# Convolution rows of all four channel blocks kept in float32 through attention, with most of their combinations made afterwards, and weight chains that begin three work units after their loads

## The chip, the cores and the metric

The program runs on one core of a Trainium2 chip. The metric is the device time of one execution in microseconds. The core has five engines with a queue each, and each works through its queue in the order in which the program was written: TensorE (PE in the profile, with its weight loads as PEld), VectorE (DVE), ScalarE (ACT), GpSimd (POOL) and SyncE (SP), which here only issues DMA transfers. An instruction that waits for another engine holds back everything behind it in its own queue.

## The reference

One layer of a hybrid encoder block on 1024 tokens of width 1024, in float32:

```
u = rms_norm(x, norm1_g)
q, k, v, cb, cc, ch, ga, gb = split(u @ w_in)        # 512 x 6, then 1024, 1024
y_a = neighbourhood_attention(norm(q), norm(k), v, rpb) @ w_attn_branch
y_b = (cb * conv3(cc * ch)) @ w_conv_branch          # 512 channels, width 3 along the tokens
x = x + (sigmoid(ga) * y_a + sigmoid(gb) * y_b) @ w_o
h = rms_norm(x, norm2_g) @ w_mlp_in
x = x + square(relu(h)) @ w_mlp_out
```

## The kernel before, in words

Every float32 operand of a large product is split into two half-precision parts, a high one and a low one, after a scaling by powers of two. A product takes three passes (high by high, high by low, low by high). For a weight this means a chain: load it, on ACT multiply by row gains and square it, sum the squares per partition on DVE, add the sums up over the partitions with a one-column matmul on PE (`all_sum`, L228 to L233), derive the scale on DVE with some small instructions (`pow2_half`), then write the high part on ACT and the low part on DVE. A chain is a generator, and each `yield` is a place where it may be set aside.

Several products save work by seven products in place of eight (`SEVEN`, `seven`). For these, the kernel forms seven sums and differences ("forms") of the four quarters of each operand, and each form is split into high and low.

The order of the instructions is written by the program itself, in stages:

- **Start (0 to about 155 us):** normalisation and the products V, Q and K.
- **Attention (to about 319 us):** 77 steps `k`. Between them PE works off the convolution products of four channel blocks, j = 0 to 3 (`conv_mms`, L1112), twelve of 128x512 each per gate and half. Each block's products are multiplied on DVE and ACT, three taps are summed (partly on POOL, L879 and L882), and the result is written to `CF` in float32 (`conv_post`). `CF` has two places, and the second half of the same tile `bT` (`STG`) holds split forms on the way to the DRAM buffer `bf`. After blocks 1 and 3, `conv_split` finds the scale of a pair and `conv_forms` makes the seven forms: the sums on POOL (L912, L928 to L937), the high parts on ACT, the low parts on POOL (L919), and transfers to `bf` (L922).
- **Gates and branches (from about 319 to 588 us):** `gate_units(n)` for eight gate blocks, `a_unit` for the attention branch, `ab(j)` for the seven products of the convolution branch, with its forms read back from `bf` into `bT` by `land` (L1441), four at a time.
- **w_o and the MLP (to the end).**

In the gate stage a **unit** (L238) writes a group of matmuls to PE's queue, mostly twelve of 512 columns, and then makes `steps` advances of the foreground generators (`fg`) and `ticks` advances of the background chains (`bg`). A tick advances the first chain of the list that doesn't answer that it waits; a chain can wait for a number of units after a mark (`apart`), so that its `all_sum` is written to PE's queue some units behind the instruction which makes its operand. `work` counts the columns of the matmuls written; 6144 of them are a unit of twelve matmuls. Where a chain isn't through when its weight is needed, `built` advances it with all these waits lifted.

The weights come through five buffers of 512 KB (`raw`), loaded in the order G0, A0, S1, B0, S2, A1, S3, B1, S4 and so on, where S is the weight of a gate block after the first, A and B those of the two branches. `load_upto` (L261) issues the next load when an earlier weight has been split. While `held` is one, a buffer is set aside for the first gate's products (`sgr`).

The chains by name: `largest` for A (a maximum, L364 to L374), `rows_scaled` (L1144), `squares` (L1153), `sum_of` (L1124 and L1125) and `scale_of` for S, `prep_b` (L1338) for B. `forms_sum` (L1270, POOL) and `parts` (L1288 high on ACT, L1284 low on DVE) make the split forms of a weight. `turn_s` (L1257) issues eight transposing transfers that the first gates need. `m_done` (L1387 to L1394) splits the merged product of a gate block.

Of the kernel before, what the change touches and what calls it, by code (L numbers as in the profile page):

```python
# [101 lines left out]
def encoder_block(ctx: ExitStack, tc: tile.TileContext, x, weights, cols, gqk, rel, masks, out):  # L102
# [160 lines left out]
    def load_upto(n):  # L263
        while loaded[0] < min(n - held[0], limit[0], len(loads)):
            ch, p = loads[loaded[0]]
            loaded[0] += 1
            t = rawp.tile([128, 1024], F32, name="raw")
            load_into(t[:, :ch.widths[p][0] * ch.widths[p][1]], ch, p)
            ch.raw.append(t)

    class Chunk:


        def __init__(self, kind, widths, tag, rows, half, more):
            self.kind, self.bank = kind, {"V": "o", "Q": "o", "K": "s", "C": "d"}.get(kind)
            self.tag, self.rows, self.widths, self.more = tag, rows, widths, more
            self.offs = []
            self.raw, self.ready, self.half, self.pool = [], more > 0, half, () if half is None else (1,)
            self.split = False
            self.fine, self.s = False, None  # L280
# [78 lines left out]
        def largest(self, rm, a, b):  # L359
            o = 0  # L360
            for p, (k, w) in enumerate(self.widths):
                while len(self.raw) <= p:
                    yield WAIT
                V.tensor_reduce(sc[:, at(rm, o, k)], self.raw[p][:, :k * w].rearrange("p (k w) -> p k w", k=k),  # L364
                                axis=AX, op=OP.max, apply_absolute_value=True)
                o += k
                yield
# [6 lines left out]
            V.tensor_copy(c, sc[:, a])  # L374
            if self.kind != "V":
                yield from apart(units[0], 3 if self.kind != "O" else 1 + (self is cO[1]))
# [471 lines left out]
    def conv_post(j, g, half, ps, d):  # L848
# [17 lines left out]
        while not d.get("taps"):  # L866
            yield
        o = CF[:, j % 2, 512 * half:512 * half + 512].rearrange("p (b r c) -> p b r c", b=4, r=16)
        V.tensor_tensor(o, p3, perm(d["cv"], half), op=OP.mult)
# [17 lines left out]
    BTF = BT.rearrange("p w j t -> p (w j t)")  # L887
    CF = BTF[:, :4096].bitcast(F32).rearrange("p (e t) -> p e t", e=2)
    STG = BTF[:, 4096:].rearrange("p (n w t) -> p n w t", n=4, w=2)
    SLOT = BTF.rearrange("p (n a w t) -> p n a w t", n=4, a=2, w=2)  # L890
    BF = dram.tile([128, 7, 2, 2, 512], F16, name="bf")
    cm, form_tail, formed = keep(2), [], [False] * 2

    def conv_split(j):
        a, e = j // 2, j % 2
        A.activation(STG[:, 3].rearrange("p w t -> p (w t)").bitcast(BF16), CF[:, e], AF.Square,
                     scale=sc[:, cConv[j].inv], accum_out=sc[:, at(cm, e)])
        yield
        if e == 0:
            return  # L900
        m, s, r = tmp(), tmp(), tmp(2)
        V.tensor_scalar(sc[:, m], sc[:, at(cm, 0)], sc[:, at(cm, 1)], 1e-36, op0=OP.add, op1=OP.max)
        yield
        yield from pow2_half(m, 14, s, at(rowsB, a))
        for i in range(2):
            mul(s, cConv[j - 1 + i].inv, at(r, i))
        form_tail.append(conv_forms(a, r))

    def conv_forms(a, r):

        for e in range(2):
            G.tensor_scalar(CF[:, e], CF[:, e], sc[:, at(r, e)], 1.0, op0=OP.mult, op1=OP.mult)  # L912
        (e0, e1), (o0, o1) = ([CF[:, e, 512 * h:512 * h + 512] for h in range(2)] for e in range(2))

        def hi(n, v):
            A.activation(STG[:, n, 0], v, AF.Copy)

        def lo(n, v):
            G.tensor_tensor(STG[:, n, 1], v, STG[:, n, 0], op=OP.subtract)  # L919

        def put(n, f):
            SP.dma_start(BF[:, f, a], STG[:, n])  # L922
        yield
        hi(0, o1), hi(1, e0), hi(2, o0)
        yield
        lo(0, o1), lo(1, e0), lo(2, o0)
        yield
        G.tensor_tensor(o1, e1, o1, op=OP.subtract)  # L928
        hi(3, o1)
        yield  # L930
        G.tensor_tensor(e1, e0, e1, op=OP.subtract)
        G.tensor_tensor(e0, o1, e0, op=OP.subtract)
        yield
        put(0, 3), put(1, 0), put(2, 1)
        lo(3, o1)
        yield
        G.tensor_tensor(o0, o0, e0, op=OP.add)  # L937
        yield
        hi(0, e1), hi(1, e0), hi(2, o0)
        put(3, 2)  # L940
        yield
        lo(0, e1), lo(1, e0)
        yield
        lo(2, o0)
        yield
        put(0, 5), put(1, 4)
        yield
        put(2, 6)
        formed[a] = True

# [177 lines left out]
    def scale_of(am, more, n=3):  # L1128
# [6 lines left out]
        return s, inv  # L1135

    def rows_scaled(ch, g):

        for i in range(2):
            while len(ch.raw) <= i:  # L1140
                yield WAIT
            for k in range(4):
                v = ch.raw[i].rearrange("p (n k c) -> p k n c", n=2, k=4)[:, k]
                A.activation(v, v, AF.Copy, scale=sc[:, at(g, 4 * i + k)])  # L1144
            yield
# [92 lines left out]
    V, A = nc.vector, nc.scalar  # L1238
    fg.extend(form_tail)
    solo[0] = False  # L1240
# [63 lines left out]
    def prep_s(n):  # L1304
# [6 lines left out]
        else:  # L1311
# [17 lines left out]
    def prep_b(j):  # L1329

        ch = cB[j]
        while not ch.raw or not formed[1]:
            yield WAIT
# [47 lines left out]
    def m_done(n):  # L1381

        m = sgr[0] if n == 0 else sgs[n][:, 0::2]
        hi, lo = (M[w][:, n].rearrange("p (h t) -> p h t", h=2) for w in range(2))
# [10 lines left out]
        merged.add(n)  # L1395
        if n == 0:
            held[0] = 0
            load_upto(done[0] + 5)

    def gate_units(n, tail=None):  # L1400
# [3 lines left out]
        if n == 0:  # L1404
            for half in (1, 0):
# [29 lines left out]

    ORDB = (1, 6, 2, 4, 5, 7, 3)

# [7 lines left out]
    def first_forms():  # L1445
        while not formed[1]:
            yield
        for g in range(4):
# [6 lines left out]
    def part(n, i):  # L1455

        return sgs[n][i] if n == 0 else sgs[n][:, i]

# [34 lines left out]
    def ab(j):  # L1493
# [3 lines left out]
        def post2():  # L1497
            V.tensor_tensor(z[0], ps[2], z[0], op=OP.add)
            times(n, 0)
# [12 lines left out]
        posts = {1: lambda: A.activation(z[0], ps[1], AF.Copy),  # L1512
                 6: lambda: V.tensor_tensor(z[1], ps[6], z[0], op=OP.add), 2: post2, 7: post7, 3: post3}

# [9 lines left out]
        if j == 0:  # L1524
            order = "bbb2bb3bb"
        o = 0
# [6 lines left out]
        pairs[0] = j + 1  # L1533

    fg.append(first_forms())
    bg.append(prep_s(1))
# [693 lines left out]
```

## Time and profile before

| | us |
|---|---|
| median of the timed runs | 1257.69 (1256.26 to 1257.75, 3 runs) |
| the profiled execution, its own time | 1257.09 |
| span from its first to its last instruction | 1255.3 |
| PE busy | 1198.5 (95%) |
| DVE busy | 956.7 (76%) |
| ACT busy | 777.6 (62%) |
| POOL busy | 504.0 (40%) |

Busy time counts an instruction's own duration. A row of the timeline gives the start, the time to the end of the merged instructions, the engine, the line, the operation, what it writes and reads, the number of instructions, and in brackets the idle time of the engine just before and what ended it. The granted clock is the share of full speed that TensorE was given. PE's durations overlap, since matmuls are pipelined: a group of twelve takes 2.75 us as a row and starts 2.59 us after the one before it.

### The profile page before, as it was taken

How to read it: one execution, taken by the hardware profiler on the slowest of the kernel's cores; microseconds unless marked ns; L12 is line 12 of the kernel's file. 1: busy time of each engine (PE TensorE's matmuls, PEld its weight loads, DVE VectorE, ACT ScalarE, POOL GpSimd, SP SyncE). 2: the span in 40 equal slices, each digit the busy share in tenths (PEclk: the TensorE clock that was granted, in tenths of full speed). 3: DMA queues.
4: the chain of work that ended last, by engine and by line, in shares of the span. 5: the costliest groups of instructions: out<-in, count | busy, mean ns of one | idle time of the engine just before them, and what ended most of it. 6: DMA issues, size and time to landing. Idle time of an engine off the chain costs nothing.

```text
span 1255.3 us, 17139 instructions
## 1 busy us (share of the span) xinstructions
PE 1198.5 (95%) x6248; PEld 577.1 (46%) x6248; DVE 956.7 (76%) x1775; ACT 777.6 (62%) x1241; POOL 504.0 (40%) x332
## 2 busy tenths in 40 slices
PE   8999999989767759999999999999999999999998
PEld 7444444445333324444447644444444444444444
DVE  7987788888455687687778765545637989999998
ACT  7774677777545753444677877778765673545430
POOL 5510022431723224030102475565557654464472
PEclk9999999999978879999999999999999999999999
DMA  7755546777544241523349455435565643526212
GB/s 259 207 148 107 116 105 129 157 172 133 128 160 156 67 156 63 168 101 126 144 78 175 159 202 185 145 133 185 180 234 216 244 183 137 199 101 251 72 63 102
DMA packets 168373, 189.62 MB, mean 151 GB/s; under 512 B 123616, under 2 KB 124128, under 8 KB 164192
## 3 DMA queue, kind: packets, MB, share of 16 engines
q1 hardware_dynamic: 168288, 188.52, 50.2%
q8 instruction: 49, 0.80, 0.3%
q14 instruction: 36, 0.29, 0.1%
HBM read 117.19 MB, written 41.42 MB: 126 GB/s over the span
## 4 chain that ended last, share of the span: by engine, by line
PE 81%; DVE 7%; ACT 5%; POOL 3%; issue 2%; DMA 1%; SPq 1%; POOLq 0%; DVEq 0%; ACTq 0%
PE ps_d L238 25%; PE ps_s L238 22%; PE ps_o L238 18%; PE ps_d L1112 6%; PE ps_d L671 2%; PE ps_d L720 2%; PE ps_s L720 2%; PE ps_s L671 1%; DVE w_s L1284 1%; PE ps_o L1093 1%; SPq L1257 1%; ACT w_s L1288 1%; PE ps_s L1017 1%; ACT raw L1144 1%; POOL raw L1356 1%
## 5 line engine op out<-in xcount | busy, mean ns | idle before, releaser
L238 PEld LDWEIGHTS <-ops 128*128 128x128 f16 x1356 | 132.5, 98 | 157.3
L238 PEld LDWEIGHTS <-w 128*128 128x128 f16 x1368 | 132.9, 98 | 139.4
L1112 PE MATMUL ps_d<-uT,w_ws 128*128 128x512 f16 x576 | 128.6, 381 | 0.0
L238 PE MATMUL ps_s<-ops 128*128 128x512 f16 (+1 forms) x528 | 119.7, 377 | 0.0
L238 PE MATMUL ps_d<-ops 128*128 128x512 f16 x480 | 110.1, 379 | 0.0
L2051 ACT ACTIVATE ops<-hf,sc 128x2048 f16<-128x2048 f32 x26 | 52.0, 1998 | 84.8 <-PE ps_s L238 37.7
L1270 POOL TENSOR_TENSOR tsum<-raw 128x512 f32<-128x512 f32 x28 | 48.2, 1739 | 139.1 <-PE ps_s L238 73.9
L238 PEld LDWEIGHTS <-w_s 128*128 128x128 f16 x588 | 57.8, 99 | 96.4 <-ACT mL L1338 18.1
L1629 POOL TENSOR_TENSOR as<-as 128x512 f32<-128x512 f32 x60 | 82.9, 1382 | 41.6 <-ACT as L1911 38.0
L1112 PEld LDWEIGHTS <-w_ws 128*128 128x128 f16 x576 | 54.7, 98 | 65.6 <-issue 1.9
L238 PE MATMUL ps_d<-u2T,w 128*128 128x512 f16 (+1 forms) x360 | 78.8, 368 | 0.0
L238 PE MATMUL ps_o<-ops 128*128 128x512 f16 (+1 forms) x348 | 78.6, 375 | 0.0
L1144 ACT ACTIVATE raw<-raw,sc 128x256 f32<-128x256 f32 x164 | 67.8, 493 | 16.4 <-DMA raw<-in_weights 14.7
L2053 DVE SCALAR_TENSOR_TENSOR ops<-hf,sc,ops 128x2048 f16<-128x2048 f32 x26 | 74.4, 2860 | 3.2 <-ACT ops L2051 2.2
L238 PE MATMUL ps_o<-u2T,w 128*128 128x512 f16 (+1 forms) x348 | 76.0, 368 | 0.0
L238 PE MATMUL ps_s<-u2x,w 128*128 128x512 f16 (+1 forms) x336 | 74.5, 371 | 0.0
L1288 ACT ACTIVATE w<-raw,sc 128x512 f16<-128x512 f32 (+1 forms) x28 | 24.6, 927 | 50.9 <-DVE sc L477 50.9
L1944 DVE TENSOR_TENSOR as<-ps_s,as 128x512 f32<-128x512 f32 x13 | 9.0, 691 | 57.9 <-ACT as L1963 57.9
L1489 POOL TENSOR_TENSOR sg<-sg 128x512 f32<-128x512 f32 x12 | 16.4, 1378 | 83.1 <-DVE sg L1479 60.5
L2067 POOL TENSOR_TENSOR raw<-raw 128x1024 f32<-128x1024 f32 x8 | 30.8, 3876 | 36.7 <-DVE ops L2061 36.7
L2025 POOL TENSOR_TENSOR t<-raw,w2x 128x1024 f32<-128x1024 f32 x6 | 18.8, 3138 | 61.8 <-DMA w2x<-in_weights 61.8
L238 PEld LDWEIGHTS <-mH 128*128 128x128 f16 x304 | 29.6, 98 | 30.4
(427 smaller groups left out, 2775.5 us busy)
## 6 DMA issues: line engine op xcount, KB each, us to landing
raw<-in_weights SPq DMA_DIRECT2D x89, 512.0 KB, 5.3
hs<-as SPq DMA_DIRECT2D x16, 1792.0 KB, 8.0
hf<-hs SPq DMA_DIRECT2D x26, 1024.0 KB, 6.4
bT<-bf SPq DMA_DIRECT2D x28, 512.0 KB, 4.6
w2x<-in_weights SPq DMA_DIRECT2D x16, 512.0 KB, 7.6
raw<-in_weights SPq DMA_DIRECT2D x16, 384.0 KB, 3.7
xt<-in_x SPq DMA_DIRECT2D x8, 512.0 KB, 11.0
gs<-s SPq DMA_DIRECT2D x4, 1024.0 KB, 4.5
```

The lines of the kernel that those rows point to most:

```text
L238: T.matmul(ps, l, r, start=a, stop=b)
L671: T.matmul(ps, UT[:, sa, k, b * 128:(b + 1) * 128], w, start=(kind, k) == ("hh", 0), stop=(kind, k) == ("hl", 7))
L720: T.matmul(vbank["q", b], UT[:, sa, k, b * 128:(b + 1) * 128], cQ.parts[:, sw, 512 * k:512 * k + 512], start=(k, n) == (0, 0), stop=(k, n) ...
L1112: T.matmul(ps, l, r, start=a, stop=b)
L1144: A.activation(v, v, AF.Copy, scale=sc[:, at(g, 4 * i + k)])
L1270: G.tensor_tensor(t[:, o], a, b, op=OP.add)
L1288: A.activation(o(0), w, AF.Copy, scale=sc[:, scale(n)])
L1629: sub.tensor_tensor(z[o], z[a], z[b], op=op)
L2025: G.tensor_tensor(T2[:, i], w12[i], w22[i], op=OP.add)
L2051: A.activation(P[:, 1, 0], hf, AF.Copy, scale=sc[:, Rs])
L2053: V.scalar_tensor_tensor(P[:, 1, 1], hf, sc[:, Rs], P[:, 1, 0], op0=OP.mult, op1=OP.subtract)
L2067: G.tensor_tensor(w11[i2], w11[i2], w12[i2], op=OP.add)
```

## The change

- `CF` takes the whole of `bT`: four float32 places, one for each block, that stay until attention is over. The scale rows of both pairs are kept (`crow`).
- Of the first pair's seven forms, three are made and stored during attention (`conv_early`), one high or low part at a time, in the space of the first K heads (`KS`). Two more sums are begun there.
- The other four forms of the first pair and all seven of the second are made after attention, in `conv_late`, as the first foreground generator of the gate stage: eleven high parts on ACT, fifteen tensor-by-tensor instructions on DVE (nine low parts, six sums), two low parts and two scalings on POOL, eleven transfers to `bf`. Their staging space is `zb` and a part of `M[1]`, and three of the four places of `zb` are used a second time.
- The chains of A, S and B begin only when three units of work have been written since their load was (`aged`); the wait between the sum and its `all_sum` grows from two units to three for S and from one to two for B, and for A it counts work in place of units.
- Eight ticks are made ahead of the gate stage (`tick(8)`).
- The first gate's products go to `sg`, and the set-aside raw buffer is given back at the end of `gate_units(0)` in place of the end of `m_done(0)`.
- The order of the convolution branch's products is 1 2 4 6 5 7 3 in place of 1 6 2 4 5 7 3, and in the first `ab` the two attention units come at places 3 and 5.

```diff
@@ load_upto @@
+            ch.when.append(work[0])
@@ Chunk.largest @@
-                while len(self.raw) <= p:
+                while len(self.raw) <= p or self.kind == "A" and not aged(self, p):
+            if self.kind == "A":
+                yield from apart(work[0], 3 * 6144, work)
@@ module level @@
-    CF = BTF[:, :4096].bitcast(F32).rearrange("p (e t) -> p e t", e=2)
+    CF = BTF.bitcast(F32).rearrange("p (e t) -> p e t", e=4)
+    KS = KD[:, 0:2].rearrange("p a w t -> p (a w t)").rearrange("p (n w t) -> p n w t", n=4, w=2)
@@ conv_early @@
+    def conv_early():
+        (e0, e1), (o0, o1) = quarters(0)
+        conv_scaled(0)
+        yield
+        yield
+        for i, v in enumerate((o1, e0, o0)):
+            hi(KS[:, i], v)
+            yield
+            lo(KS[:, i], v, G)
+            yield
+        G.tensor_tensor(o1, e1, o1, op=OP.subtract)
+        yield
+        G.tensor_tensor(e1, e0, e1, op=OP.subtract)
+        for i, f in enumerate((3, 0, 1)):
+            put(KS[:, i], f, 0)
+            yield
@@ conv_late @@
+    def conv_late():
+        zs = zb.rearrange("p n t -> p (n t)").bitcast(F16).rearrange("p (n w t) -> p n w t", n=4, w=2)
+        ms = M[1][:, 2:6].rearrange("p n (w t) -> p n w t", w=2)
+        (e0, e1), (o0, o1) = quarters(0)
+        V.tensor_tensor(e0, o1, e0, op=OP.subtract)
+        V.tensor_tensor(o0, o0, e0, op=OP.add)
+        conv_scaled(1)
+        hi(zs[:, 0], o1), hi(zs[:, 1], e1)
+        yield
+        (p0, p1), (q0, q1) = quarters(1)
+        V.tensor_tensor(zs[:, 0, 1], o1, zs[:, 0, 0], op=OP.subtract)
+        V.tensor_tensor(zs[:, 1, 1], e1, zs[:, 1, 0], op=OP.subtract)
+        hi(zs[:, 2], e0), hi(zs[:, 3], o0)
+        yield
+        lo(zs[:, 2], e0, V), lo(zs[:, 3], o0, V)
+        yield
+        put(zs[:, 0], 2, 0), put(zs[:, 1], 5, 0)
+        hi(ms[:, 0], q1), hi(ms[:, 1], p0), hi(ms[:, 2], q0)
+        yield
+        put(zs[:, 2], 4, 0), put(zs[:, 3], 6, 0)
+        formed[0] = True
+        lo(ms[:, 0], q1, V), lo(ms[:, 1], p0, G), lo(ms[:, 2], q0, G)
+        V.tensor_tensor(q1, p1, q1, op=OP.subtract)
+        yield
+        yield
+        V.tensor_tensor(p1, p0, p1, op=OP.subtract)
+        V.tensor_tensor(p0, q1, p0, op=OP.subtract)
+        hi(ms[:, 3], q1)
+        yield
+        put(ms[:, 0], 3, 1), put(ms[:, 1], 0, 1), put(ms[:, 2], 1, 1)
+        V.tensor_tensor(q0, q0, p0, op=OP.add)
+        hi(zs[:, 0], p1), hi(zs[:, 1], p0)
+        yield
+        lo(ms[:, 3], q1, V), lo(zs[:, 0], p1, V)
+        hi(zs[:, 2], q0)
+        yield
+        lo(zs[:, 1], p0, V), lo(zs[:, 2], q0, V)
+        yield
+        put(ms[:, 3], 2, 1), put(zs[:, 0], 5, 1)
+        yield
+        put(zs[:, 1], 4, 1), put(zs[:, 2], 6, 1)
+        formed[1] = True
@@ aged @@
+    def aged(ch, i):
+        return forced[0] or i >= len(ch.when) or work[0] >= ch.when[i] + 3 * 6144
@@ rows_scaled @@
-            while len(ch.raw) <= i:
+            while len(ch.raw) <= i or ch.kind == "S" and not aged(ch, i):
@@ prep_s @@
-            s, ch.inv = yield from scale_of(am, 9, 2)
+            s, ch.inv = yield from scale_of(am, 9, 3)
@@ prep_b @@
-        while not ch.raw or not formed[1]:
+        while not ch.raw or not rowed[0] or not aged(ch, 0):
-        s, ch.inv = yield from scale_of(am, 0, 1)
+        s, ch.inv = yield from scale_of(am, 0, 2)
@@ m_done @@
-        if n == 0:
-            held[0] = 0
-            load_upto(done[0] + 5)
@@ gate_units @@
-                A.activation(sgr[0][:, half], sgr[0][:, half], AF.Sigmoid)
-            return [sgr[0][:, 0], z[1], sgr[0][:, 1], z[3]]
+                A.activation(z[2 * half], sgr[0][:, half], AF.Sigmoid)
+            held[0] = 0
+            load_upto(done[0] + 5)
+            return sg
@@ ORDB @@
-    ORDB = (1, 6, 2, 4, 5, 7, 3)
+    ORDB = (1, 2, 4, 6, 5, 7, 3)
@@ first_forms @@
-        while not formed[1]:
-            yield
+        yield from conv_late()
@@ ab @@
-            order = "bbb2bb3bb"
+            order = "bb2b3bbbb"
@@ before the first gate @@
+    tick(8)
     fg.append(first_forms())
```

More of the change, by code (lines that the diff above doesn't have):

```diff
@@ L277, in __init__ @@
             self.offs = []
+            self.when = []
             self.raw, self.ready, self.half, self.pool = [], more > 0, half, () if half is None else (1,)
@@ L374, in largest @@
             V.tensor_copy(c, sc[:, a])
-            if self.kind != "V":
+            if self.kind == "A":
+                yield from apart(work[0], 3 * 6144, work)
+            elif self.kind != "V":
                 yield from apart(units[0], 3 if self.kind != "O" else 1 + (self is cO[1]))
@@ L867, in conv_post @@
             yield
-        o = CF[:, j % 2, 512 * half:512 * half + 512].rearrange("p (b r c) -> p b r c", b=4, r=16)
+        o = CF[:, j, 512 * half:512 * half + 512].rearrange("p (b r c) -> p b r c", b=4, r=16)
         V.tensor_tensor(o, p3, perm(d["cv"], half), op=OP.mult)
@@ L905, in conv_split @@
         for i in range(2):
-            mul(s, cConv[j - 1 + i].inv, at(r, i))
-        form_tail.append(conv_forms(a, r))
-    def conv_forms(a, r):
-        for e in range(2):
[L912 to L922, printed above, removed]
+            mul(s, cConv[j - 1 + i].inv, at(crow, i))
@@ new lines, in conv_split, with conv_scaled, hi, lo @@
+        if a == 0:
+            form_tail.append(conv_early())
+        else:
+            rowed[0] = True
+    def conv_scaled(a):
+        for e in range(2):
+            t = CF[:, 2 * a + e]
+            G.tensor_scalar(t, t, sc[:, at(crow, e)], 1.0, op0=OP.mult, op1=OP.mult)
+    def hi(t, v):
+        A.activation(t[:, 0], v, AF.Copy)
+    def lo(t, v, e):
+        e.tensor_tensor(t[:, 1], v, t[:, 0], op=OP.subtract)
+    def put(t, f, a):
+        SP.dma_start(BF[:, f, a], t)
+    def conv_early():
+        (e0, e1), (o0, o1) = quarters(0)
+        conv_scaled(0)
@@ L1238, in encoder_block @@
     V, A = nc.vector, nc.scalar
-    fg.extend(form_tail)
+    assert not form_tail and rowed[0]
     solo[0] = False
@@ L1455, in part @@
     def part(n, i):
-        return sgs[n][i] if n == 0 else sgs[n][:, i]
+        return sgs[n][:, i]
     def a_unit(n, half):
```

34 lines of the change are left out of this document (10 added, 24 removed).

## The prediction

> **What bounds the kernel now.** First the page's span, then the busy time by stages (columns: window, length, busy time of PE, PEld, DVE, ACT and POOL with counts, granted clock, DMA share, GB/s).
>
> ```profile
> span 1255.3 us, 17139 instructions
> ```
>
> ```profile
> 319.00:396.00 77.00, 52.55 (x230) 22.84 (x229) 40.28 (x78) 40.87 (x76) 30.97 (x25) 0.84 0.53 158
> 396.00:476.00 80.00, 60.62 (x266) 26.34 (x264) 58.40 (x126) 44.75 (x77) 27.00 (x21) 0.87 0.37 116
> 476.00:588.00 112.00, 111.88 (x520) 50.57 (x519) 83.09 (x161) 47.56 (x76) 29.21 (x24) 1.00 0.28 89
> ```
>
> PE is the bound, and from 476 to 588 it is full. From 319 to 476, in the stage that the change edits, it isn't: 113 of 157 us, at a granted clock of 0.84 and 0.87. So I read PE's timeline there next:
>
> ```profile
> 334.52 2.75 PE L238 MATMUL ps_d<-uT,w_s 128*128 128x512 f16 x12
> 355.07 0.16 PE L229 MATMUL ps_s<-ones 128*128 128x1 bf16 x1 [17.80 <-DVE ones L1125]
> 355.10 4.39 PE L238 MATMUL ps_d<-qD,w_s 128*128 128x512 f16 x12
> ...
> 381.88 1.47 PE L238 MATMUL ps_o<-bT,w_wb 128*128 128x512 f16 x6 [1.62 <-DMA bT<-bf]
> 388.37 0.16 PE L229 MATMUL ps_d<-ones 128*128 128x1 bf16 x1 [5.03 <-DVE ones L1125]
> 388.40 4.80 PE L238 MATMUL ps_s<-qD,w_wa 128*128 128x512 f16 x12
> ...
> 425.86 0.16 PE L229 MATMUL ps_s<-ones 128*128 128x1 bf16 x1 [6.61 <-DVE ones L374]
> 425.89 4.83 PE L238 MATMUL ps_o<-uT,w_s 128*128 128x512 f16 x12
> ...
> 440.96 1.46 PE L238 MATMUL ps_s<-bT,w_wb 128*128 128x512 f16 x6
> ...
> 459.08 0.16 PE L229 MATMUL ps_s<-ones 128*128 128x1 bf16 x1 [12.78 <-DVE ones L1125]
> 459.10 2.72 PE L238 MATMUL ps_d<-bT,w_wb 128*128 128x512 f16 x6
> 461.62 4.06 PE L238 MATMUL ps_s<-qD,w_wa 128*128 128x512 f16 x12
> ```
>
> Four of the five waits stand at a one-column `all_sum` (L229): it was written to PE's queue before DVE had made its operand, and ready products stand behind it. After each of these four, a group of twelve takes 4.06 to 4.83 us in place of 2.75, and one of six 2.72 in place of 1.46. Until 396 that makes 17.80 + 1.62 + 5.03 = 24.4 of waiting and 1.6 + 2.1 = 3.7 of slow groups, 28 together; after 396, 6.61 + 12.78 = 19.4 and 2.1 + 1.3 + 1.3 = 4.7, 24 together. Dense, the two stages would last 77 − 28 = 49 and 80 − 24 = 56 us. So **52 us** is all that can be had here. What was late in the wait of 17.80 is seen on ACT and in SP's queue:
>
> ```profile
> 349.17 1.70 ACT L1144 ACTIVATE raw<-raw,sc 128x256 f32<-128x256 f32 x4 [6.84 <-DMA raw<-in_weights]
> ...
> 353.00 0.71 ACT L1338 ACTIVATE mL<-raw,sc 128x512 bf16<-128x512 f32 x1
> ```
>
> ```profile
> 332.60 11.22 SPq L1257 DMA_TRANSPOSE uT<-gs  x8
> 343.91 0.52 SPq L922 DMA_DIRECT2D bf<-bT  x1
> 344.55 0.87 SPq L261 DMA_DIRECT2D raw<-in_weights  x2
> ```
>
> B0's squares (L1338) sat on ACT behind the row scaling of S2, which waited for a load that SP issued at 344.55, behind eight transposes. The wait of 12.78 is of another kind. There DVE was at work:
>
> ```profile
> 456.13 2.64 DVE L1284 SCALAR_TENSOR_TENSOR w_s<-gsum,sc,w_s 128x1024 f16<-128x1024 f32 x2
> 458.69 0.15 DVE L1124 TENSOR_REDUCE sc<-sc 128x1 f32<-128x2 f32 x1
> 458.87 0.16 DVE L1125 CAST ones<-sc 128x1 bf16<-128x1 f32 x1
> ```
>
> B2's sum lay behind the low parts of an S weight that isn't used before 476: a backlog, not a transfer.
>
> **The change, part by part.**
>
> *Ages and longer waits.* With `aged`, S2's scaling is written three units after its load, so B0's squares pass it; the `all_sum` of B and of S is written a unit later. A unit is 2.6 us, so DVE may now be 5.2 (B) or 7.8 us (S) behind PE. No instruction is added. Behind 476 I take them at nothing: PE's 111.88 of 112 covers DVE's 83.09. Without this cover they cost a forced chain, priced under D.
>
> *`tick(8)` and the raw buffer.* A0's split (326.00 in a row below) moves ahead of the gates, some 7 us sooner, and its successor's load with it; the fifth buffer is free at the end of the first gate, not after `m_done(0)`. But S1's two buffers are still read by POOL's four sums behind two scalings (1.2 us each, by the `bT` row below) and by a low part, so the next two loads stand on SP until some 9 us after the gates' start, ahead of the transposes.
>
> *The late forms.* Rows: the first gate stage for instructions on `bT` alone (busy PE, DVE, ACT, POOL), the stores' time to landing, and three of DVE:
>
> ```profile
> 319.00:396.00 77.00, 9.73 (x42) 0.00 (x0) 4.19 (x7) 14.65 (x12) 0.84 0.53 158
> ```
>
> ```profile
> bf<-bT SPq DMA_DIRECT2D x7, 256.0 KB, 4.7
> ```
>
> ```profile
> 326.00 4.66 DVE L332 SCALAR_TENSOR_TENSOR w_wa<-raw,sc,w_wa 128x256 f16<-128x256 f32 x4 [8.70 <-ACT w_wa L345]
> ...
> 383.79 0.69 DVE L1513 TENSOR_TENSOR zb<-ps_s,zb 128x512 f32<-128x512 f32 x1 [4.81 <-ACT zb L1512]
> 384.40 1.66 DVE L332 SCALAR_TENSOR_TENSOR w_wa<-raw,sc,w_wa 128x256 f16<-128x256 f32 x4
> ```
>
> POOL does twelve instructions of forms there now, 14.65 us; afterwards four, about 5. ACT does four high parts more, 4.19 / 7 = 0.6 each: 2.4. DVE gets fifteen, at 0.69 each 10.4 us. With both inputs in SBUF they have no clean row: below, 0.69; above, beside POOL, 0.69 + (4.66 − 1.66) / 4 = 1.44. I take 0.69, since POOL's own load falls by 10. So DVE has 40.28 + 10.4 = 50.7 us of work in a stage which dense would last 49: **DVE becomes the bound of the first stage**.
>
> Nor will it run through. The stores of `conv_late`'s fourth advance follow the transposes on SP, 9 + 2 (two loads) + 11.22 = 22 us after the gates' start, and land 4.7 later, at 27. ACT overwrites the same places of `zb` in the eighth advance, which it reaches at about 16 by its own work. It stands for eleven us, and DVE, which needs those high parts next, for some 7. Behind it on ACT are S2's scaling and squares and one more high part (6 us), on DVE the last low parts and then A1's column, ready at about 34. PE comes to A1's `all_sum` after eleven units, at 28.5. So **what is late next is A1's sum**, 5.5 us and a slow group of 1.6. The last forms are stored from 34, landed at 39 and read back, at the same 4.7, at 44; the first product that needs them stands after thirteen units, at 34 dense and at 41 behind this wait. It was at 53:
>
> ```profile
> 372.32 1.46 PE L238 MATMUL ps_d<-bT,w_wb 128*128 128x512 f16 x6
> ```
>
> I take 64 us for the first stage: 50.7 of DVE, 7 of its standing and 6 for its shorter waits on ACT and POOL. Bounds: 49 (dense) and 77 (nothing won).
>
> In the second stage DVE's 58.40 are above the dense 56. But five S weights were split between 319 and 476:
>
> ```profile
> L1284 DVE SCALAR_TENSOR_TENSOR w_s<-gsum,sc,w_s 128x1024 f16<-128x1024 f32 x10 | 13.7, 1389 | 4.2 <-ACT w_s L1288 4.2
> ...
> L1284 DVE SCALAR_TENSOR_TENSOR w_s<-raw,sc,w_s 128x1024 f16<-128x1024 f32 x5 | 7.4, 1482 | 0.9 <-ACT w_s L1288 0.9
> ```
>
> S5's is due only after gate 4, which begins at 476. With ages and longer waits its (13.7 + 7.4) / 5 = 4.2 us and what goes with it leave the stage: some 53 for 56, in bursts. I take 66 (bounds 56 and 80).
>
> The 4.66 speaks against the change: four low parts, each held up beside POOL. The Trainium skill (SBUF — State Buffer, Who interferes with whom) says why: a DVE instruction with two SBUF inputs and a GpSimd instruction that reads SBUF shut each other out for a whole instruction, whichever starts first. The row agrees with it. By that rule each of the fifteen can wait out one POOL instruction, but only eight run near them (two scalings, four sums of S1, two low parts), which keeps the loss below 8 × 1.2 = 10 us, where rival C has 11.
>
> *Attention.* There POOL makes thirteen instructions of the first pair's forms, and afterwards seven. PE's waits there on DVE's `sc`, from 232 to 319:
>
> ```profile
> PE ps_s L1017 <- DVE sc L97: 4.8, 3, 1.8
> ```
>
> At most 4.8 us go, and at least none, since the seven left still meet the taps and biases on POOL. I take 3. The `sg` tile and the order of the products cost nothing: the same instructions, under PE.
>
> **Sum.** 77 − 64 = 13, 80 − 66 = 14, attention 3: 30 us. The profiled execution took 1257.09 (its span and 1.8 around it), 0.6 below the median, so **1227 us**.
>
> **The rivals.**
>
> *B, all the waits go.* For it: all but one have one form, and 476 to 588 has none of it. DVE's 50.7 then set the first stage: 26 + 24 + 5 = 55 less, 1202. Against: the reuse of `zb`.
>
> *C, DVE is shut out.* The fifteen go at 1.44: 11 us more, the first stage lasts 75; half of that backlog goes over, the second lasts 72. With 2 from attention 12 less, 1245. For it: the 4.66. Against: eight POOL instructions fewer.
>
> *D, slower: chains run into force.* The place is `built(cS[2])` ahead of gate 2. Counted in units from the gates' start, with the ticks that each gives, S2's sum is written at 10, its `all_sum` at 13, its last low part by 16.5; gate 2 begins at 18.5. If B0's chain or a load not yet aged holds it for over two units, the waits are lifted and PE stands for the rest: scaling 2 × 1.70, squares 4 × 0.71, POOL's sums 4 × 1.2, high parts 7 × 0.6, slow group 2.1, 17 us in all. S2 and S3 both forced cost 34, more than the 30 won: 1261. For it: each of these chains grows by three or four units, with five buffers to feed them. Against: the count.
>
> *E, no effect.* Other sums of the same backlog stall PE as long: 1257.
>
> **How the numbers follow.** Forecast (1216 to 1238) 0.42, B 0.18, C 0.22, E 0.06, D 0.12. Faster by over 0.2% (2.5 us, what a measurement can tell from no change) is forecast, B and C, 0.82; same 0.06; slower 0.12. The range leaves out D, the far side of E and the end of B: 1204 to 1252.
>
> **What would show it.** Right: no wait near 17 us in the first gates, but one near 5 at A1's `all_sum` (operand of L374), with ACT idle on `bf` before it; DVE above 75% of the first stage; the first convolution product 41 to 45 us after the first gate's start, now 53; PE's waits on DVE in attention below 2. Wrong: DVE's form instructions stretched to 1.4 (C); an `all_sum` wait of over 10 just ahead of gate 2 or 3 (D); ACT not idle on `bf` at all (B).

## The result, and the profile after

The changed kernel takes 1241.36 us (median of 4 runs, 1240.20 to 1244.53), the kernel before, timed beside it, 1257.12: a ratio of 0.988, with an interval of 0.986 to 0.990. The forecast was 1227, its range 1204 to 1252. The sign was right; of the 30 us foreseen 16 came.

First the span of the changed kernel, then its busy time in the three stages (columns as in the prediction's table by stages; the stages begin 4, 11 and 22 us sooner than before).

```profile
span 1239.4 us, 17137 instructions
```

```profile
314.60:384.00 69.40, 54.07 (x226) 22.97 (x225) 51.51 (x89) 44.55 (x84) 20.68 (x17) 0.88 0.66 199
384.00:454.00 70.00, 58.54 (x267) 25.78 (x265) 49.64 (x110) 40.92 (x67) 25.73 (x20) 0.94 0.33 109
454.00:566.00 112.00, 108.96 (x494) 48.58 (x494) 82.91 (x172) 45.78 (x73) 30.85 (x25) 0.98 0.27 91
```

The stages are bounded by four rows of PE's timeline: the first product of the gates, of gate 2, of gate 4 and of w_o. In the kernel before they are

```profile
318.98 3.19 PE L238 MATMUL ps_o<-uT,w_ws 128*128 128x512 f16 x14
...
395.65 1.67 PE L238 MATMUL ps_d<-uT,w_s 128*128 128x512 f16 x7
...
475.95 2.32 PE L238 MATMUL ps_d<-uT,w_s 128*128 128x512 f16 x10
...
587.82 0.59 PE L238 MATMUL ps_s<-w_ws,mH 128*128 128x512 f16 x2
```

and in the changed kernel, with PE's longer waits between them:

```profile
314.65 5.34 PE L238 MATMUL ps_o<-uT,w_ws 128*128 128x512 f16 x24
...
333.56 0.16 PE L229 MATMUL ps_d<-ones 128*128 128x1 bf16 x1 [3.21 <-DVE ones L1169]
...
346.97 0.18 PE L229 MATMUL ps_d<-ones 128*128 128x1 bf16 x1 [1.35 <-DMA bf<-mL]
...
358.24 0.19 PE L229 MATMUL ps_s<-ones 128*128 128x1 bf16 x1 [3.24 <-DVE sc L232]
358.29 2.72 PE L238 MATMUL ps_d<-bT,w_wb 128*128 128x512 f16 x6
...
381.72 2.74 PE L238 MATMUL ps_d<-bT,w_wb 128*128 128x512 f16 x6 [7.53 <-DMA bT<-bf]
...
384.33 1.94 PE L238 MATMUL ps_o<-uT,w_s 128*128 128x512 f16 x8
...
425.09 0.16 PE L229 MATMUL ps_s<-ones 128*128 128x1 bf16 x1 [6.83 <-DVE ones L376]
...
453.97 5.28 PE L238 MATMUL ps_d<-uT,w_s 128*128 128x512 f16 x12 [4.12 <-DVE zb L1549]
...
477.96 2.75 PE L238 MATMUL ps_o<-uT,w_s 128*128 128x512 f16 x12 [2.27 <-DVE sg L1478]
...
571.89 0.59 PE L238 MATMUL ps_s<-w_ws,mH 128*128 128x512 f16 x2
```

| part | before, us | after, us | gain | foreseen gain |
|---|---|---|---|---|
| up to the gates | 318.98 | 314.65 | 4.3 | 3 |
| first stage | 76.7 | 69.7 | 7.0 | 13 |
| second stage | 80.3 | 69.6 | 10.7 | 14 |
| gate 4 to w_o | 111.9 | 117.9 | −6.1 | 0 |

The sum is 15.9, and the two profiled executions differ by 1257.09 − 1241.13 = 16.0. The waits of 17.80 and 12.78 us are gone, and smaller ones stand at other places. Two of those are at no sum at all: 7.53 us for a read-back of the convolution's forms (`bT`), and 4.12 us for DVE's reading of a PSUM bank at the start of gate 4.

How the 7.53 us come about is told by the chain that ended last, over this stretch (start, us, what; the longer pieces between the two ends):

```profile
354.18 3.75 DVE w_wb L1331 x3
...
357.99 3.56 DMA raw<-in_weights
...
361.63 1.71 ACT raw L1191 x4
...
367.93 2.70 ACT w_s L1335 x3
...
370.63 4.68 DVE w_s L1331 x3
375.31 1.58 DVE w_wa L334 x4
```

with SP's queue beside it:

```profile
357.99 0.33 SPq L261 DMA_DIRECT2D raw<-in_weights  x1
...
369.39 7.86 SPq L261 DMA_DIRECT2D raw<-in_weights  x3
377.34 7.47 SPq L1487 DMA_DIRECT2D bT<-bf  x5
```

A load for S3 goes out when DVE has read B0's buffer (357.9). ACT's scaling waits for this load, though its chain is aged: `aged` counts from where the load is *written*, and the load itself stood on SP for its buffer. Behind the scaling on ACT stand the high parts of the S weight split at that time, behind these DVE's low parts, behind these three buffers, behind the buffers three loads on SP, and behind the loads the read-backs that PE needs.

### The profile page after: what moved, and what is told of

Same layout as the page of the kernel before. It is cut to its first block, busy times and chain, and to the rows that moved or that the text cites. A ratio compares the mean times of both kernels' runs of the same rounds, so it can differ in the third digit from the quotient of the medians.

```text
span 1239.4 us, 17137 instructions
## 1 busy us (share of the span) xinstructions
PE 1199.1 (97%) x6248; PEld 576.3 (46%) x6248; DVE 963.5 (78%) x1790; ACT 778.1 (63%) x1241; POOL 486.0 (39%) x317
## 4 chain that ended last, share of the span: by engine, by line
PE 79%; DVE 10%; ACT 5%; POOL 2%; DMA 1%; issue 1%; SPq 1%; ACTq 0%; POOLq 0%; DVEq 0%
PE ps_d L238 24%; PE ps_s L238 20%; PE ps_o L238 18%; PE ps_d L1156 9%; PE ps_d L675 2%; PE ps_d L724 2%; PE ps_s L724 2%; PE ps_s L675 1%; DVE w_wb L1331 1%; PE ps_o L1137 1%; DVE w_s L1331 1%; PE ps_s L1061 1%; ACT w_s L1335 1%; POOL raw L1403 1%; POOL sg L1534 1%
## 5 line engine op out<-in xcount | busy, mean ns | idle before, releaser
L1534 POOL TENSOR_TENSOR sg<-sg 128x512 f32<-128x512 f32 x14 | 19.9, 1433 | 116.2 <-DVE sc L232 52.9
## 6 DMA issues: line engine op xcount, KB each, us to landing
xt<-in_x SPq DMA_DIRECT2D x8, 512.0 KB, 11.2
```

The costliest lines, as they stand in the source:

```text
L1534: G.tensor_tensor(t, t, part(n, 2 * half + 1), op=OP.add)
```

## The experiments

Each was timed beside the kernel before on the same chip (medians 1256.65 to 1257.46). "Waits" is the sum of PE's waits of 0.4 us and more between 240 and 650 us of the profiled execution, added up from its timeline.

| kernel | us | ratio to before, interval | waits |
|---|---|---|---|
| before | 1257.12 | 1 | 48.6 |
| changed | 1241.36 | 0.988 (0.986 to 0.990) | 31.9 |
| a1_ages_alone | 1260.37 | 1.0030 (1.0019 to 1.0041) | 49.6 |
| a2_no_ages | 1257.12 | 1.0003 (0.9993 to 1.0012) | 45.5 |
| a5_ages_buffer | 1252.85 | 0.9968 (0.9956 to 0.9981) | 42.7 |
| a6_ages_forms | 1249.64 | 0.9933 (0.9914 to 0.9952) | 41.1 |
| a3_lands_first | 1244.66 | 0.9904 (0.9888 to 0.9920) | 33.1 |
| a4_a_waits_5 | 1243.92 | 0.9902 (0.9883 to 0.9921) | 34.0 |
| a7_late_pool | 1241.63 | 0.9875 (0.9860 to 0.9890) | 32.8 |
| a8_turn_later | 1237.57 | 0.9848 (0.9829 to 0.9867) | 30.7 |
| a9_loads_lag2 | 1241.13 | 0.9874 (0.9857 to 0.9890) | 31.7 |
| b2_after_lag2 | 1238.92 | 0.9861 (0.9846 to 0.9876) | 29.2 |
| c0_s4_out | 1241.59 | 0.9885 (0.9869 to 0.9902) | 30.9 |
| c1_raw6 | 1249.25 | 0.9943 (0.9927 to 0.9959) | 38.9 |

### The change in three parts

The change has three parts: the ages with the longer waits; the buffer (the early `tick(8)`, the `sg` tile, the raw buffer given back at the end of the first gate); the forms (`conv_early`, `conv_late`, the order of products). Two kernels came first. The ages alone, in the kernel before:

```
-                while len(self.raw) <= p:
+                while len(self.raw) <= p or self.kind == "A" and not aged(self, p):
...
-            while len(ch.raw) <= i:
+            while len(ch.raw) <= i or ch.kind == "S" and not aged(ch, i):
...
-            s, ch.inv = yield from scale_of(am, 9, 2)
+            s, ch.inv = yield from scale_of(am, 9, 3)
```

> The kernel before with the ages (S rows, B, A begin three units behind their loads) and the longer waits alone; its convolution forms, its order of products and its raw buffers are untouched. Theory 1 (the delayed chains take the waits away): the 17.80 us at B0's sum and the 12.78 us at B2's go, each to under 5, and most of the 15.8 us that the whole change gains come with this part, 1243 to 1247. Theory 2 (the late forms make the gain, because they free ACT and POOL ahead of the gates): waits of over 10 stay, 1254 to 1258. Theory 3 (the two only work together: with the old forms DVE, ACT and POOL are as late as before, so the delayed chains come later still): slower than 1257.

and everything but the ages, in the changed kernel:

```
-        return forced[0] or i >= len(ch.when) or work[0] >= ch.when[i] + 3 * 6144
+        return True
...
-            s, ch.inv = yield from scale_of(am, 9, 3)
+            s, ch.inv = yield from scale_of(am, 9, 2)
```

> The changed kernel without the ages and with the old waits (S 2, B 1, A counted in units); forms, raw buffer, early tick and order of products stay changed. Theory 1: the wait of B0's sum is near 15 again, and one of over 8 stands ahead of gate 3; 1250 to 1257. Theory 2: it stays within 3 us of 1241. Theory 3: slower than 1257, since DVE's fifteen new instructions then queue behind chains that wait for their loads.

Measured: the ages alone lose 0.3% (+3.6 us), the rest alone neither wins nor loses. Theories 1 and 2 fall; neither part brings the gain by itself. Theory 3 is right that the two only work together, but a2 is no slower than the kernel before. In a1 PE's timeline shows

```profile
339.24 0.60 PE L238 MATMUL ps_s<-qD,w_s 128*128 128x512 f16 x2 [2.41 <-ACT w_s L1295]
341.91 3.76 PE L238 MATMUL ps_s<-qD,w_s 128*128 128x512 f16 x10 [2.06 <-DVE w_s L1291]
...
403.87 0.16 PE L229 MATMUL ps_o<-ones 128*128 128x1 bf16 x1 [12.82 <-DVE ones L1129]
...
493.04 0.16 PE L229 MATMUL ps_s<-ones 128*128 128x1 bf16 x1 [14.44 <-DVE ones L1129]
```

and ACT's

```profile
335.06 2.05 ACT L920 ACTIVATE bT<-bT 128x512 f16<-128x512 f32 x3 [4.17 <-DMA bf<-bT]
337.02 2.17 ACT L1295 ACTIVATE w_s<-gsum,sc 128x1024 f16<-128x1024 f32 x2
```

The wait of 17.80 is away, as theory 1 says, but PE now waits for the weights themselves. The old forms hold ACT 4.17 us for a store, and the high parts of gate 1's weight, due at once, stand behind. This isn't new: in the kernel before ACT stands 4.22 us at the same place, but PE is then still at B0's sum. With 14.44 us at a sum behind gate 4, the sum of waits is what it was. Two further kernels give the ages one partner each. The ages and the buffer, with the old forms:

```
+            held[0] = 0
+            load_upto(done[0] + 5)
+            return sg
...
+    tick(8)
     fg.append(first_forms())
```

> The kernel before with the ages and longer waits, and with the early tick(8), the sg tile and the raw buffer given back at the end of the first gate; the convolution forms and the order of the products stay as before. The ages alone gave 1260.4, all the rest without the ages 1257.1, both together 1241.4, so the ages need a partner. Theory P (the partner is the buffer: a chain that begins three units behind its load needs that load early, and with four buffers until m_done(0) it is not): 1242 to 1247. Theory Q (the partner is the forms: with the old forms ACT and POOL are the late engines, and an early buffer only brings the wait elsewhere): 1256 to 1262.

and the ages and the forms, with the buffer as before:

```
+        if n == 0:
+            held[0] = 0
+            load_upto(done[0] + 5)
...
-            held[0] = 0
-            load_upto(done[0] + 5)
             return sg
...
-    tick(8)
     fg.append(first_forms())
```

> The changed kernel without the early tick(8) and with the raw buffer given back behind m_done(0) as before; ages, late forms and order stay. Theory P: the loads of the first gates come late again, waits on w_s or at an all_sum of over 8 appear, 1254 to 1260. Theory Q: within 4 us of 1241.

Both kernels lie between their two theories: both partners count. With the ages in place, the buffer is worth 0.6% without the new forms (1.0030 to 0.9968) and 0.5% with them (0.9933 to 0.9879), some 7 us; the forms 1.0% and 0.9% (1.0030 to 0.9933, 0.9968 to 0.9879), 11 to 12 us. Without the ages the two together are worth nothing. Which half of the buffer's part works, the tick or the release, these runs don't tell.

### One wait taken away

Loads held back during `ab(0)`, so that the read-backs pass them on SP:

```
+        if j == 0:
+            limit[0] = loaded[0]
...
+        if j == 0:
+            limit[0] = 10 ** 6
+            load_upto(done[0] + 5)
         pairs[0] = j + 1
```

> The changed kernel with its weight loads held back during ab(0) and released right behind it, so that on SP the read-backs of the convolution's forms no longer stand behind loads that wait for a raw buffer. Theory: the 7.53 us wait of PE for bT at the end of ab(0) goes to under 1 and its slow group with it; the loads come some 4 us later, which the units to their due hide: 1232 to 1235. Rival: the S and A chains behind are late by what the loads are, and a wait of 5 or more appears at an all_sum ahead of gate 3: 1239 to 1244.

A's `all_sum` two units later:

```
-                yield from apart(work[0], 3 * 6144, work)
+                yield from apart(work[0], 5 * 6144, work)
```

> The changed kernel with A's all_sum five units behind its column instead of three. Theory (the 6.83 us at A2's sum and the 1.35 at A1's come from the backlog on DVE, not from a missing load): both go, and a slow group of 1.8; A's split comes two units later and is still in time: 1231 to 1235. Rival: the backlog only shows at the next sum or at the next PSUM bank (the 4.12 for zb grows to 8 or more): 1239 to 1243. Second rival: A's high and low parts come too late for their product, a wait on w_wa of 3 or more: over 1243.

In both the wait aimed at went, and the time didn't fall. In a3 PE waited 3.96 and 8.36 us at the next sums in its place, in a4 8.83 at the sum of a B weight, as the rivals had it; both times (1244.66 and 1243.92) lie a little above the rivals' ranges, and the intervals overlap with that of the changed kernel. DVE and ACT do the same work, and what comes next in PE's queue meets it late.

Nine low parts of the late forms on POOL instead of DVE:

```
-        lo(zs[:, 2], e0, V), lo(zs[:, 3], o0, V)
+        lo(zs[:, 2], e0, G), lo(zs[:, 3], o0, G)
...
```

> The changed kernel with nine of the fifteen late instructions of the convolution forms on POOL instead of DVE (the low parts; the six sums stay on DVE). Theory R (as forecast: DVE's own work bounds the first stage): DVE loses 9 x 0.69 = 6 us and the stage gets 4 to 6 us shorter, 1235 to 1238. Theory S (no engine's sum bounds the stage, each stands in turn for another; POOL's nine at 1.2 lie in the same chain and lock DVE out more often): the first product on bT comes some 5 us later and the time is 1243 to 1250.

The time stays (1241.63), against both theories, and so does the length of the stage. Its row, and two of the six sums that stayed on DVE:

```profile
314.60:384.00 69.40, 51.27 (x226) 22.15 (x224) 49.79 (x80) 44.44 (x84) 31.88 (x26) 0.88 0.65 196
```

```profile
L956 DVE TENSOR_TENSOR bT<-bT 128x512 f32<-128x512 f32 x1 | 1.6, 1640 | 0.0
L974 DVE TENSOR_TENSOR bT<-bT 128x512 f32<-128x512 f32 x1 | 1.6, 1626 | 2.6 <-POOL mL L929 2.6
```

DVE gave up 9 × 0.69 = 6.2 us and its busy time fell by only 51.51 − 49.79 = 1.7, mostly because four of the six sums, with POOL at work, now take 1.46 to 1.64 (in the changed kernel one of the six did, 1.54). So this run doesn't tell whether less DVE work would help.

The eight transposes behind the first four stores:

```
-                if half:
-                    turn_s(0, 2)
                 A.activation(z[2 * half], sgr[0][:, half], AF.Sigmoid)
+            turn_s(0, 2)
             held[0] = 0
```

> The changed kernel with the eight transposes of turn_s(0, 2) written behind the first four stores of the late forms instead of ahead of them. Theory (as forecast: the reuse of zb is what ACT and DVE stand for in the first stage): the stores go out at about 14 us after the gates' start instead of 23, ACT's 4.37 us and DVE's 2.65 and 3.65 for bf and zb go, the first product on bT comes 5 to 8 us earlier; of this the wait at B0's sum (3.21) and the two of S2 and A1 (4.6) are won, 1233 to 1237. Rival: the transposes are now late for gate 1, which waits for uT by 4 or more: 1241 to 1246. Second rival: the stage is as long and the waits only stand elsewhere: 1239 to 1243.

This kernel has the lowest time of the study, 3.8 us below the changed one (the intervals of the ratios still overlap, by 0.0008). The four stores in SP's queue, and PE at the end of `ab(0)`:

```profile
327.20 2.52 SPq L932 DMA_DIRECT2D bf<-zb  x4
```

```profile
377.93 2.74 PE L238 MATMUL ps_d<-bT,w_wb 128*128 128x512 f16 x6 [10.92 <-DMA bT<-bf]
```

The stores go out 12.5 us after the gates' start, ACT no longer waits for them, and the first product on `bT` comes 4.6 us sooner (353.66 in place of 358.29). The waits at S2's and A1's sums (3.24 and 1.35) are gone, and no wait for `uT` came. But the wait at B0's sum stays at 3.21, and the wait for `bT` grew by 10.92 − 7.53 = 3.4, because PE arrives sooner. With 1237.57 the gain is just short of the theory's 1233 to 1237. The first stage by the table of stages:

```profile
314.60:380.50 65.90, 51.63 (x228) 22.33 (x226) 51.34 (x89) 44.33 (x84) 21.09 (x17) 0.90 0.69 212
```

It has the same DVE work (51.34 us) in 65.9 us in place of 69.4: DVE's sum was not what set its length.

On a8, and then on the changed kernel, every load was written two units later:

```
         units[0] += 1
+        load_due(units[0])
...
     def load_upto(n):
+        if lag[0]:
+            pend.append((units[0] + lag[0], n, work[0]))
...
+    lag[0] = 2
     tick(8)
```

> The kernel a8_turn_later with every weight load of the gate stages written two units after the point at which it is written now, so that SP stands less for a raw buffer that DVE still reads, and the read-backs of the forms get past; the ages still count from the old point. Theory (head of the line: the 10.92 us that PE waits for bT at the end of ab(0) are SP's standing of 7.86 us for raw buffers ahead of five read-backs): that wait falls by 5 to 11, the loads land when they did because the buffer and not the issue sets them, 1228 to 1233. Rival (as in a3_lands_first, where the wait for bT went and 3.96 and 8.36 appeared at the next sums): the late chains of S and B take what is won, 1236 to 1241.

> The same late writing of the loads in the changed kernel itself, with turn_s(0, 2) where it is. Theory: as a9, the 7.53 us for bT falls by 5 or more, 1233 to 1237. Rival: 1240 to 1245, as with a3_lands_first.

In both the wait for `bT` went altogether (10.92 and 7.53 us). But a9 lies 3.6 us above a8, and b2 only 2.4 below the changed kernel, where the theory gave 4 to 8; in both pairs the intervals of the ratios overlap. In a9 PE stands instead at a sum

```profile
379.80 0.16 PE L229 MATMUL ps_s<-ones 128*128 128x1 bf16 x1 [6.58 <-DVE ones L1182]
```

and on DVE that sum follows the same low parts that had held up the loads:

```profile
373.76 3.48 DVE L1344 SCALAR_TENSOR_TENSOR w_s<-gsum,sc,w_s 128x1024 f16<-128x1024 f32 x2
...
379.59 0.16 DVE L1182 CAST ones<-sc 128x1 bf16<-128x1 f32 x1
```

So the read-back in a8 and the sum in a9 stand behind the same late split on DVE; taking the first wait away uncovers the second.

### A sixth buffer

Is that split late because there are too few raw buffers? To make room for a sixth, `s4T` and its four transposes are left out first, and the products that read it read another form, so that the outputs are not the reference's:

```
-    s4T = w3p.tile([128, 2, 4, 512], F16, name="s4T", bufs=1)
...
-            lambda s: UT[:, s, 4:8, 512:1024], free(0), free(2), lambda s: s4T[:, s]]
+            lambda s: UT[:, s, 4:8, 512:1024], free(0), free(2), lambda s: UT[:, s, 4:8, 0:512]]
```

> The changed kernel without the s4T tile and its four transposes; the products that read s4T read the second form of u in its place, so the outputs are not the reference's. It makes room for c1_raw6 and is its comparison. All theories: within 3 us of 1241, since the transposes stand on SP ahead of loads that wait for a raw buffer anyway, and the products are the same in number and shape.

```
-        while loaded[0] < min(n - held[0], limit[0], len(loads)):
+        while loaded[0] < min(n - held[0] + six(), limit[0], len(loads)):
...
+            if six(ch) and turn6[0] % 6 == 1:
+                t = extra[0].tile([128, 1024], F32, name="raw6", bufs=1)
```

> c0_s4_out with a sixth raw buffer for the S, A and B weights from the end of the first gate on, and one load more ahead. Theory U (five raw buffers set the pace: a4, a3, a9, b2 and a7 each took a wait away and the sum of PE's waits stayed at 29 to 34 us, and giving a buffer back early was worth 8 us with both kinds of forms): SP's standing for raw buffers shrinks, PE's waits between 314 and 480 fall from 29 to under 20 and the time to 1228 to 1235. Theory W (the order in which the chains stand on ACT, DVE and POOL sets it, and the loads are there in time): waits 27 or more, within 3 us of c0_s4_out.

c0 takes as long as the changed kernel (1241.59). The sixth buffer makes it 7.7 us *slower* (1249.25), which neither theory had. At the place itself it does what it should: ACT scales S3 in one go, where the changed kernel waits 5.08 us for the load. First c1, then the changed kernel:

```profile
353.90 3.28 ACT L1203 ACTIVATE raw<-raw,sc 128x256 f32<-128x256 f32 x8
```

```profile
361.63 1.71 ACT L1191 ACTIVATE raw<-raw,sc 128x256 f32<-128x256 f32 x4 [5.08 <-DMA raw<-in_weights]
```

But two of PE's waits in c1 are longer than in the changed kernel:

```profile
382.68 2.74 PE L238 MATMUL ps_o<-bT,w_wb 128*128 128x512 f16 x6 [11.93 <-DMA bT<-bf]
...
414.88 0.16 PE L229 MATMUL ps_o<-ones 128*128 128x1 bf16 x1 [10.82 <-DVE sc L1180]
```

A1's four low parts, which took 1.58 in the chain above, now meet POOL's sums for the next S weight. DVE and POOL in c1:

```profile
373.09 4.68 DVE L346 SCALAR_TENSOR_TENSOR w_wa<-raw,sc,w_wa 128x256 f16<-128x256 f32 x4
...
410.36 2.29 DVE L1338 SCALAR_TENSOR_TENSOR w_wb<-raw,sc,w_wb 128x256 f16<-128x256 f32 x2
412.57 1.20 DVE L378 TENSOR_REDUCE sc<-raw 128x4 f32<-128x1024 f32 x1
```

```profile
373.25 1.44 POOL L1324 TENSOR_TENSOR gsum<-raw 128x512 f32<-128x512 f32 x1 [2.36 <-DVE w_s L1338]
```

so the loads that wait for A1's buffer stand 3 us longer on SP (10.88 in place of 7.86). At 414.88 PE waits for a sum, as far as the rows show that of A2: its maximum (L378) stands on DVE behind B1's low parts. So in this kernel loads that come earlier are no gain by themselves: what they start can go ahead of what is due, and beside what it slows.

## Why the prediction was right, and where it failed

The range held and the sign was right, but the size was not: the first and second stage gave 7.0 and 10.7 us in place of 13 and 14, and 6.1 were lost behind them. Of the signs named, three came (no wait near 17, ACT idle on `bf`, the first product on `bT` in time) and three didn't (a wait near 5 at A1's sum, DVE above 75% of the first stage, PE's waits in attention below 2).

**Attention, 3 foreseen, 4.3 measured.** PE's waits on DVE's `sc` fell from 5.3 us (the 4.8 of the prediction's row and two short ones) to 2.6 (1.88, 0.22 and 0.51), and the gates begin 4.3 us sooner. Where the other 1.6 us come from was not traced.

**The late forms' course: right in order, off in sizes.** SP's stores were put at 22 us after the gates' start, and are at 337.62 − 314.65 = 23.0. ACT, DVE and SP there:

```profile
340.06 1.33 ACT L926 ACTIVATE zb<-bT 128x512 f16<-128x512 f32 x2 [4.37 <-DMA bf<-zb]
```

```profile
340.73 1.40 DVE L929 TENSOR_TENSOR zb<-bT,zb 128x512 f16<-128x512 f32 x2 [2.65 <-ACT zb L926]
345.77 0.69 DVE L929 TENSOR_TENSOR zb<-bT,zb 128x512 f16<-128x512 f32 x1 [3.65 <-ACT zb L926]
...
346.76 0.16 DVE L376 CAST ones<-sc 128x1 bf16<-128x1 f32 x1
```

```profile
337.62 2.06 SPq L932 DMA_DIRECT2D bf<-zb  x4
```

ACT stood 4.37 us and not 11: it reached the place at 21 us, not 16, and the stores let it go 2.4 us after their issue began, not 4.7. Of the 5 us by which ACT came late, it stood 3.60 for DVE's first sum, behind A0's four low parts, which took 5.17 us beside POOL's four sums. So that DVE's standing came out near the forecast is in part luck. DVE stood 2.65 + 3.65 = 6.3 (foreseen 7), A1's column was there at 32.1 (foreseen 34), the first product on `bT` at 358.29 − 314.65 = 43.6 (foreseen 41, sign 41 to 45). That the transposes ahead of these stores cost time is what a8 points to (3.8 us, with intervals that overlap).

**"DVE becomes the bound of the first stage": its work was right, the conclusion wrong.** 51.51 us of DVE work against 50.7 foreseen, but 74% of the stage, with 18 us of standing in place of 7 + 6. The step that failed is the term "6 for its shorter waits on ACT and POOL": these came to 17.9 − 6.3 = 11.6 us. One wait alone was 5.31, for the high parts which stood on ACT behind the scaling that waited 5.08 us for S3's load:

```profile
368.57 0.75 DVE L1331 SCALAR_TENSOR_TENSOR w_s<-raw,sc,w_s 128x512 f16<-128x512 f32 x1 [5.31 <-ACT w_s L1335]
```

The prediction followed SP's queue as far as the first stores and took the read-backs behind them as free to go; that loads waiting for a buffer stand ahead of read-backs was missing. PE's wait of 7.53 us and the slow group behind it (2.74 for 1.46) come of this. They don't by themselves explain the 6 us by which the stage was missed: without this wait b2 is only 2.4 us faster, and a3 isn't faster at all.

**The second stage, 66 foreseen, 69.6 measured: S5's split did not leave it.** The prediction took 4.2 us of low parts "and what goes with it" out of this stage. But five S weights are still split ahead of gate 4, in the same twenty low parts on DVE as before, and PE's wait of 4.12 us stands right behind the fifth. DVE's last low part for it waits for ACT's high part and that for POOL's sums, and behind it DVE reads the PSUM bank that PE waits for:

```profile
441.57 3.79 DVE L1331 SCALAR_TENSOR_TENSOR w_s<-raw,sc,w_s 128x512 f16<-128x512 f32 x2 [0.73 <-ACT w_s L1335]
...
449.92 1.28 DVE L1331 SCALAR_TENSOR_TENSOR w_s<-gsum,sc,w_s 128x1024 f16<-128x1024 f32 x1 [2.34 <-ACT w_s L1335]
...
453.24 0.68 DVE L1549 TENSOR_TENSOR zb<-ps_d,zb 128x512 f32<-128x512 f32 x1
```

DVE's work fell all the same, further than foreseen (58.40 to 49.64 us in place of 53), in part because A2's four low parts took 1.68 us where they had taken 4.70. At 71% of the stage it wasn't what set the length. PE's waits of 6.83, 0.51 and 4.12 and the slow group behind the first (4.57 for 2.75) are 13.3 us, which is nearly all that lies between the dense 56 and 69.6.

**A1's sum as the next late thing** was foreseen at 5.5 + 1.6; it is 1.35, with no slow group. In its place three waits of the same kind stand at B0's sum (3.21), S2's (3.24) and, in the second stage, A2's (6.83). The kind was right, the place not.

**"Behind 476 I take them at nothing": wrong, 6.1 us.** The cover was read off a stage in which PE had no wait; now gate 4 begins with the wait of 4.12 (counted in the second stage) and goes on with a group at 5.28 in place of 2.75 and waits of 2.27 and less, all on DVE. That the ages cost something here is seen in the parts: a1, a5 and a6, with ages, have waits of 14.44, 9.20 and 14.43 us in this stage, a2, without them, none above 0.24.

**The sum by parts.** The working took the ages as the source of most of both stages' gain, and the forms and the buffer as terms of their own. a1 and a2 show that the parts don't add up: +3.6, 0, and together −16. The ages need the forms out of ACT's way and the buffer early; forms and buffer need the ages.

**The rivals.** C (1245) is nearest in time, but not in cause: fourteen of the fifteen late instructions on DVE ran at 0.69, one at 1.54. The price of working beside POOL stands at other places: A0's four low parts (5.17 us against 1.66 for A1's at 375.24), B0's three, 3.75 us in the chain above against 0.51 for one alone (352.51 in the trace), and in a7 and c1. By the Trainium skill (SBUF — State Buffer, Who interferes with whom) a DVE instruction with two SBUF inputs and a GpSimd instruction that reads SBUF contend for one port pair, an exclusive lock. These rows agree with it. D's mechanism, chains that hold a weight back from its gate, did not show in the changed kernel, which has no wait of 0.4 us on `w_s`; a1 has six such waits, the longest of 2.41 us, where D reckoned with 17 at a time. B fell with the reuse of `zb`.

**What stays open.** The eight kernels with the whole change and five buffers have waits of 29 to 34 us, whichever single one was removed, while PE, DVE and ACT are busy for 84%, 71% and 59% of the changed kernel's second stage. That the order of the chains on ACT, DVE and POOL sets this is what a3, a4, a9 and c1 point to; no run changed that order as a whole, so it isn't shown. Why the early buffer gains 7 us and a sixth one loses 8 is explained by rows only for c1.

## What to carry to other kernels

Where several in-order queues feed one another, removing the wait that the profile names uncovers the next one behind the same late work: follow the chain of waits back to its origin before pricing a wait at its length, and expect a good part of it to come back at the next sum, read-back or PSUM bank. Ask of a delay that is counted from where a load is written whether the load itself can go out then, and ask of every queue what stands ahead of the transfer that is needed next. Parts of such a change should be timed together and apart, since here neither half was worth anything without the other.

## What the runs showed of the hardware that was not expected

A wait cost more than its length: the six products behind the wait of 7.53 us took 2.74 in place of 1.46, the twelve behind 4.12 took 5.28 in place of 2.75, so that 1.3 and 2.5 us more belong to their price. The granted clock of these two groups (381.72 to 384.30 and 453.97 to 459.10) was 0.50; behind the wait of 2.27 us (477.96 to 480.50) it was 1.00, and the group took 2.75. From the gates on, in the changed kernel, each wait of 3.21 us and more is followed by a slow group, and none of 2.27 us and less. The other runs set no sharp line between: behind a wait of 3.24 us a9 has a group of six at 1.46, behind one of 2.87 a2 has twelve at 4.40.

Moving two-input work from DVE to POOL relieved DVE of only 1.7 of 6.2 us, while POOL's busy time rose by 31.88 − 20.68 = 11.2. The first of four stores of 256 KB let its source go 2.4 us after its issue, where the median to landing before was 4.7.
